# A recurrence of small matmuls woven into a projection: one burst instead of two halves in six of nine steps

## The chip, the cores and the metric

The kernel runs on one core of one Trainium2 chip. The time is device microseconds from the start to the end of one execution. Lower is better.

## The reference

One layer of a streaming encoder. 16 learned meta tokens are put ahead of 512 real tokens, the rows are RMS-normalised, and one projection `P = hn @ w_in` makes 8320 columns. Half of them feed an RWKV-7 time mixing with 16 heads of 64, the other half a gated short convolution. Both results are put side by side, go through an output projection, are added to the residual and normalised once more. The part that matters here is the recurrence, per head:

```
def step(S, inp):
    r_t, w_t, k_t, v_t, kk_t, b_t = inp
    sa = einsum('bhvk,bhk->bhv', S, kk_t)
    S = S * w_t[:, :, None, :] - sa[..., None] * b_t[:, :, None, :] + v_t[..., None] * k_t[:, :, None, :]
    y_t = einsum('bhvk,bhk->bhv', S, r_t)
    return S, y_t
```

The result `y` is then normalised per head (mean, variance), scaled and gated.

## The kernel before

The input projection is a long stream of big matmuls on TensorE: 128x128 weights against 256 to 272 or 512 columns. Every weight quarter of 512 columns is split into a high part (`nc.scalar.copy`, L149, on ScalarE) and a low part (`tensor_tensor` subtract, L150, on VectorE), and three products per weight block make up the precision. The split parts live in a pool of six buffers (`bufs=6`), so each split waits until TensorE has used up an older quarter.

TensorE's order is written out by hand, in the order in which the code issues its matmuls. The stream is a generator, `flow`; `fill(ns)` takes big matmuls from it until their costs (0.43 ns for each column) sum to at least `ns`. Everything else, the recurrence among it, is put between such fills, so that its waits lie under big matmuls. On ScalarE, VectorE, GpSimd and the DMA queue of SyncE a scheduler orders the instructions by priority, so that a change of TensorE's order can change theirs.

The recurrence (`recur`) is done in chunks of 64 tokens: nine steps, `c` from 0 (the meta tokens) to 8, with `NCH = 9`. All 16 heads go together, as 64x64 matmuls that each use a quarter of the array. One step is, in the order of TensorE:

- `rz` (L1036): products with the old state `st` and with the values. ScalarE copies the result to `pn`.
- `fill(FW["p"])`, 2900 ns of big matmuls.
- `rz` (L1053): a product with the inverse that was prepared before. ScalarE and VectorE copy the result to `u` (L1056, L1057).
- `fill(FW["u"])`, 2900 ns.
- the burst: `zs` (the update of the state, L1091) and `zy` (the output, L1095, with a part of it in `rz` at L1091) are issued in turn. In a step with both it has 160 matmuls of 64x64.
- VectorE makes the new state, `st = (zs + st) * decay` (L1103, L1104), and `norm` reduces and normalises `zy` (L1120 to L1132).
- `fill(FW["s"])`, 4200 ns, and then the next step, whose first matmuls read `st`.

In steps 1 to 7 a further `fill(FW["mid"])`, 1000 ns, stands in the middle of the burst. Steps 0 and 8 have no such fill; there the 1000 ns are added to the one after the burst:

```
if c and not last and n == steps_ // 2:
    fill(FW["mid"])
...
fill(FW["s"] if c and not last else FW["s"] + FW["mid"])
```

After the recurrence the rest of the stream runs on, and then the output projection (L1334), a Strassen-like scheme whose right-hand sides `o` are split in the same way (L1302, L1303).

Of the kernel before, what the change touches and what calls it, by code (L numbers as in the profile page):

```python
# [25 lines left out]
NCH = SEQ // CH + 1  # L26
# [16 lines left out]
FW = dict(  # L43
    evac=34, start=1062, lora=2200, gram=8800, meta={0: 2000}, gram_b=13500, gram2=5500, misc=2000, v=2000, vt=1000, solve=24500, more={0: 5500, 2: 2400},
    tr=3200, lev=3000, cp=4200, out=1500, begin=19500, p=2900, u=2900, s=4200, mid=1000, last=3700, mix=2600,
)
# [43 lines left out]
def hymba_kernel(ctx: ExitStack, tc: tile.TileContext, xt, xtok, front, w_in, w_out, pv, lup, cst, msk, gf, out):  # L90
# [512 lines left out]
    def step():  # L603
        t = next(flow, None)
        if t is None:
            run_pending(float("inf"))
        else:
            clock[0] += t
            run_pending(clock[0])
        return t  # L610

    def fill(ns):
        while ns > 0:
            seen = len(ready)
            t = step()
            if t is None:
                return
            ns -= t
            if len(ready) > seen:
                ns += FW["evac"]  # L620
# [23 lines left out]
    def ahead():  # L644
        return tc.high_priority(offset=AHEAD)
# [367 lines left out]
    def load_chunk(ch, c, pairs, ops):  # L1013
        n = OPW if c < NCH - 1 else O_B
        for i in pairs:
            t = ch.tile([P, OPW], F32, tag=f"ct{i}", name=f"ct{i}_{c}", bufs=2)
            nc.sync.dma_start(t[:, 0:n], spot(i, 0, P, c, 1, 1, 0, n))
            ops[c, i] = t
# [3 lines left out]
    def recur(ch):  # L1022
        ops = {}
        load_chunk(ch, 0, range(NPAIR), ops)
        load_chunk(ch, 1, range(NPAIR), ops)
        st = None
        for c in range(NCH):
            last = c == NCH - 1
            z = [pz.tile([P, 2, 4, CH], F32, tag="tz", name=f"rz{c}_{e}") for e in range(2)]
            for k in range(4):  # L1030
                for part in range(0 if c else 1, 2):
                    for e in range(2):
                        t = ops[c, 2 * k + e]
                        o = O_KK if part else O_AR
                        for h, hs, ho in heads:
                            nc.tensor.matmul(  # L1036
                                z[e][ho if e else hs, 0, k], t[hs, o : o + CH],
                                t[hs, O_V : O_V + CH] if part else st[hs, 4 * e + k],
                                start=(part == 0 or c == 0), stop=(part == 1),
                            )  # L1040
            pn = ch.tile([P, 2, 4, CH], F32, tag="pn", name=f"pn{c}", bufs=2)
            with ahead():
                for e in range(2):
                    nc.scalar.activation(pn[:, e], z[e][:, 0], AF.Copy, scale=-1.0)
            if c and not last:
                load_chunk(ch, c + 1, range(4, NPAIR), ops)
            fill(FW["p"])
            for k in range(4):
                for e in range(2):
                    t = ops[c, 2 * k + e]  # L1050
                    for h, hs, ho in heads:
                        m = ho if e else hs
                        nc.tensor.matmul(z[e][hs, 1, k], t[m, O_X : O_X + CH], pn[m, e, k], start=True, stop=True)  # L1053
            u = ch.tile([P, 2, 4, CH], F32, tag="u", name=f"u{c}", bufs=2)
            with ahead():
                nc.scalar.copy(u[:, 0], z[0][:, 1])  # L1056
                nc.vector.tensor_copy(u[:, 1], z[1][:, 1])  # L1057
            fill(FW["u"])
            here, there = [], []
            if not last:  # L1060
                zs = pi.tile([P, NPAIR, CH], F32, tag="misc", name=f"zs{c}")
            if c:
                zy = pi.tile([P, NPAIR - 1, CH], F32, tag="ser", name=f"zy{c}")
            for k in range(4):
                for e in range(2):
                    t, j = ops[c, 2 * k + e], 4 * e + k
                    if not last:
                        bb = t[:, O_B : O_B + 2 * CH].rearrange("p (s a) -> p a s", a=2)
                        here += [(zs, j, bb[:, 0], 0, u[:, e, k], 0, 2), (zs, j, bb[:, 1], 0, t[:, O_V : O_V + CH], 1, 2)]
                    if c and j < NPAIR - 1:  # L1070
                        there += [
                            (zy, j, st[:, j], O_AR + CH, t, 0, 3),
                            (zy, j, t[:, O_V : O_V + CH], O_KK + CH, t, 1, 3),
                            (zy, j, u[:, e, k], O_BR, t, 2, 3),
                        ]
                    elif c:

                        here += [
                            (z[0][:, 0], 0, t, O_AR + CH, st[:, j], 0, 3),
                            (z[0][:, 0], 0, t, O_KK + CH, t[:, O_V : O_V + CH], 1, 3),  # L1080
                            (z[0][:, 0], 0, t, O_BR, u[:, e, k], 2, 3),
                        ]
            steps_ = max(len(here), len(there))
            for n in range(steps_):
                if c and not last and n == steps_ // 2:
                    fill(FW["mid"])
                if n < len(here):
                    d, j, t, o, x, a, b = here[n]
                    for h, hs, ho in heads:
                        w = t[hs, o : o + CH] if o else t[hs]  # L1090
                        nc.tensor.matmul(d[hs, j], w, x[hs], start=(a == 0), stop=(a == b - 1))  # L1091
                if n < len(there):
                    d, j, x, o, t, a, b = there[n]
                    for h, hs, ho in heads:
                        nc.tensor.matmul(d[ho, j], t[hs, o : o + CH], x[hs], start=(a == 0), stop=(a == b - 1))  # L1095
            if c + 2 < NCH:
                load_chunk(ch, c + 2, range(0, 4), ops)
            if not last:
                new = ch.tile([P, NPAIR, CH], F32, tag="st", name=f"st{c}", bufs=2)
                scale = dd[:, c].unsqueeze(2).to_broadcast([P, NPAIR, CH])  # L1100
                with ahead():
                    if c:
                        nc.vector.tensor_tensor(out=new, in0=zs, in1=st, op=ALU.add)  # L1103
                    nc.vector.tensor_tensor(out=new, in0=new if c else zs, in1=scale, op=ALU.mult)  # L1104
                st = new
            if c:
                norm(ch, (zy, z[0][:, 0, 0:1]), c)
            fill(FW["s"] if c and not last else FW["s"] + FW["mid"])


    def norm(ch, zs, c):
# [40 lines left out]
    with tc.tile_pool(name="ch", bufs=1, side="right", reuse_waits="tile") as ch:  # L1152
        recur(ch)
# [463 lines left out]
```

## Time and profile before

| | |
|---|---|
| runs | 1000.02, 1000.05, 998.6 us; median 1000.02 us |
| profiled execution | 998.63 us, of which the span of instructions is 996.8 us |
| TensorE (PE) busy | 987.4 us, 99% of the span, 9767 matmuls |
| VectorE (DVE) busy | 710.1 us, 71% |
| ScalarE (ACT) busy | 389.9 us, 39% |
| GpSimd (POOL) busy | 124.6 us, 12% |
| mean granted TensorE clock | 0.998 |
| the recurrence, first to last small matmul | 623.9 to 772.5 us after the start |

PE stands for the matmuls and PEld for the loads of their weights, which overlap the matmul before. A matmul's duration runs over the start of the next one, so that the time that the stream needs is read from the distance of starts, not from the sum of durations. A merged row of the timeline ("x8") gives the start of its first instruction.

### The profile page before, as it was taken

The numbers are of one execution on the slowest core, as the hardware profiler recorded it, in microseconds if no ns is written. First come the engines' busy times: TensorE is split into PE (matmuls) and PEld (weight loads), VectorE is DVE, ScalarE is ACT, GpSimd is POOL, SyncE is SP. The second block draws the span as 40 slices with busy tenths as digits, with TensorE's granted clock in tenths as the row PEclk, the third lists the DMA queues.
The fourth block names the chain that finished last, engine by engine and source line by source line (L and its number), as shares of the span: only waits on it lengthen the run. The fifth ranks groups of instructions, "written<-read, shape, count | busy, mean of one in ns | idle before, by whom it ended". The sixth has DMA issues, their size and how long they took to land.

```text
span 996.8 us, 23828 instructions
## 1 busy us (share of the span) xinstructions
PE 987.4 (99%) x9767; PEld 911.1 (91%) x9767; DVE 710.1 (71%) x1404; ACT 389.9 (39%) x722; POOL 124.6 (12%) x234
## 2 busy tenths in 40 slices
PE   9999999999999999999999999999999999999996
PEld 9999999999998999998999998889889898788885
DVE  7777966688666678754787754455565698998897
ACT  7553422344313434323434322222232335546464
POOL 0110201102011111010111000011211102001001
PEclk9999999999999999999999999999999999999999
DMA  9426586446754374744375837777773697697654
GB/s 324 154 89 156 136 211 164 140 127 147 198 156 156 98 197 114 194 141 132 88 182 125 207 111 224 266 240 215 202 248 87 164 284 201 185 308 198 149 127 168
DMA packets 185148, 174.82 MB, mean 175 GB/s; under 512 B 121488, under 2 KB 142800, under 8 KB 184528
## 3 DMA queue, kind: packets, MB, share of 16 engines
q1 hardware_dynamic: 182448, 164.40, 56.8%
q0 software_dynamic: 2304, 8.39, 4.7%
q8 instruction: 76, 1.25, 0.5%
q10 hardware_dynamic: 288, 0.52, 0.1%
q14 instruction: 32, 0.26, 0.1%
HBM read 136.92 MB, written 36.35 MB: 174 GB/s over the span
## 4 chain that ended last, share of the span: by engine, by line
PE 95%; DVE 3%; issue 1%; ACT 0%; DMA 0%; DVEq 0%; POOL 0%; ACTq 0%
PE ps_v L350 9%; PE ps_h L350 9%; PE ps_C L350 9%; PE ps_B L365 9%; PE ps_g L350 9%; PE ps_gc L365 9%; PE ps_k L350 8%; PE ps_r L350 8%; PE M L1334 5%; PE P L1334 4%; PE Q L1334 2%; PE g L742 2%; PE ps_k L365 1%; PE zy L1095 1%; DVE o L1303 1%; PE ps_r L365 1%
## 5 line engine op out<-in xcount | busy, mean ns | idle before, releaser
L149 ACT CAST w<-wr 128x512 fp32r<-128x512 f32 x252 | 154.0, 619 | 295.5 <-PE ps_C L350 46.2
L150 DVE TENSOR_TENSOR w<-wr,w 128x512 fp32r<-128x512 f32 x252 | 178.2, 716 | 111.8 <-ACT w L149 111.1
L350 PE MATMUL ps_v<-xh,w 128*128 128x256 f32 (+2 forms) x512 | 84.1, 285 | 0.0
L365 PE MATMUL ps_B<-xh,w 128*128 128x512 f32 x256 | 83.6, 395 | 0.0
L350 PE MATMUL ps_h<-xh,w 128*128 128x256 f32 (+2 forms) x512 | 81.8, 281 | 0.0
L365 PE MATMUL ps_gc<-xh,w 128*128 128x512 f32 x256 | 81.7, 393 | 0.0
L350 PE MATMUL ps_C<-xh,w 128*128 128x256 f32 (+2 forms) x512 | 81.5, 281 | 0.0
L350 PE MATMUL ps_g<-xh,w 128*128 128x256 f32 (+2 forms) x512 | 81.5, 281 | 0.0
L350 PEld LDWEIGHTS ps_v<-xh,w 128*128 128x128 f32 x512 | 73.9, 188 | 0.3
L350 PE MATMUL ps_k<-xh,w 128*128 128x256 f32 (+1 forms) x448 | 73.6, 285 | 0.0
L350 PE MATMUL ps_r<-xh,w 128*128 128x256 f32 (+1 forms) x448 | 72.8, 281 | 0.0
L350 PEld LDWEIGHTS ps_h<-xh,w 128*128 128x128 f32 x512 | 72.0, 189 | 0.3
L350 PEld LDWEIGHTS ps_C<-xh,w 128*128 128x128 f32 x512 | 72.0, 189 | 0.4
L350 PEld LDWEIGHTS ps_g<-xh,w 128*128 128x128 f32 x512 | 72.0, 189 | 0.3
L350 PEld LDWEIGHTS ps_k<-xh,w 128*128 128x128 f32 x448 | 64.8, 188 | 0.4
L350 PEld LDWEIGHTS ps_r<-xh,w 128*128 128x128 f32 x448 | 63.6, 189 | 0.2
L350 PE MATMUL ps_h<-xl,w 128*128 128x256 f32 x256 | 56.9, 281 | 0.0
L365 PEld LDWEIGHTS ps_gc<-xh,w 128*128 128x128 f32 x256 | 47.7, 188 | 10.0
L365 PEld LDWEIGHTS ps_B<-xh,w 128*128 128x128 f32 x256 | 47.8, 188 | 9.6
L350 PE MATMUL ps_C<-xl,w 128*128 128x256 f32 x256 | 56.2, 280 | 0.0
L350 PE MATMUL ps_v<-xl,w 128*128 128x256 f32 x256 | 55.8, 278 | 0.0
L350 PE MATMUL ps_g<-xl,w 128*128 128x256 f32 x256 | 55.5, 278 | 0.0
(367 smaller groups left out, 2183.8 us busy)
## 6 DMA issues: line engine op xcount, KB each, us to landing
wr<-in_w_in_dram SPq DMA_DIRECT2D x126, 512.0 KB
ct<-opd SPq DMA_DIRECT2D x64, 288.0 KB
wo<-in_w_out_dram SPq DMA_DIRECT2D x24, 512.0 KB
x<-in_w_out_dram POOLq DMA_DIRECT2D x16, 512.0 KB, 5.7
opd<-ar SPq DMA_DIRECT2D x8, 576.0 KB
opd<-gt SPq DMA_DIRECT2D x16, 288.0 KB
opd<-bt SPq DMA_DIRECT2D x64, 64.0 KB
x<-in_w_out_dram SPq DMA_DIRECT2D x8, 512.0 KB
```

The costliest lines, as they stand in the source:

```text
L149: nc.scalar.copy(hi, rq)
L150: low[q] = eng.tensor_tensor(out=lo, in0=rq, in1=hi.bitcast(F32), op=ALU.subtract).ins
L350: nc.tensor.matmul(ps[r][:, 0 : b - a], ww[:, k * P : (k + 1) * P], xx[:, kt, a:b], start=(kt == 0 and n == 0), stop=(kt == KT - 1 and n = ...
L365: nc.tensor.matmul(ps[r], ww[:, w], xx[:, kt, a:b], start=(kt == 0 and n == 0), stop=(kt == KT - 1 and n == 2))
L742: nc.tensor.matmul(z[h][:, c - c0], bk[hs, c, h : h + 2, :].rearrange("p a s -> p (a s)"), ar[hs, c].rearrange("p a s -> p (a s)"), start= ...
L1095: nc.tensor.matmul(d[ho, j], t[hs, o : o + CH], x[hs], start=(a == 0), stop=(a == b - 1))
L1303: last = nc.vector.tensor_tensor(out=lo, in0=rq, in1=hi.bitcast(F32), op=ALU.subtract)
L1334: nc.tensor.matmul(bank[s], left(prod, jj, m, s), w, start=(jj == 0 and n == 0), stop=(jj == 7 and n == 2))
```

## The change

The fill in the middle of the burst is kept in step 7 alone (`c == NCH - 2`, the last step before the shorter last one). In steps 1 to 6 the 1000 ns move into the fill behind the burst, which asks for 5200 ns in one piece instead of 1000 and 4200.

```diff
             for n in range(steps_):
-                if c and not last and n == steps_ // 2:
+                if c == NCH - 2 and n == steps_ // 2:
                     fill(FW["mid"])
...
             if c:
                 norm(ch, (zy, z[0][:, 0, 0:1]), c)
-            fill(FW["s"] if c and not last else FW["s"] + FW["mid"])
+            fill(FW["s"] if c == NCH - 2 else FW["s"] + FW["mid"])
```

On TensorE, in the middle of the burst of step 1 (`zs` and `zy` are the burst, `ps_B` is a tile of the big stream, `st` the old state, `ct` and `u` operands of the step):

```order
@@ -2916,8 +2916,4 @@
 L1091 MATMUL zs_8670<-ct_1_8356 64x64 x2
 L1095 MATMUL zy_8671<-st_8507,ct_1_8354 64x64 x2
-L365 MATMUL ps_B_0_8562<-xh,w_8312 128x512
-L365 MATMUL ps_B_0_8562<-xh,w_8315 128x512
-L365 MATMUL ps_B_0_8562<-xl,w_8315 128x512
-L365 MATMUL ps_B_0_8562<-xh,w_8315 128x512 x2
 L1091 MATMUL zs_8670<-u_8653,ct_1_8358 64x64 x2
 L1095 MATMUL zy_8671<-ct_1_8354 64x64 x2
```

Five big matmuls leave the burst, and its two halves of 80 small ones now follow each other directly. At the end of the same burst, on TensorE:

```order
@@ -2940,4 +2936,8 @@
 L1095 MATMUL zy_8671<-ct_1_8360 64x64 x2
 L1095 MATMUL zy_8671<-u_8653,ct_1_8360 64x64 x2
+L365 MATMUL ps_B_0_8562<-xh,w_8312 128x512
+L365 MATMUL ps_B_0_8562<-xh,w_8315 128x512
+L365 MATMUL ps_B_0_8562<-xl,w_8315 128x512
+L365 MATMUL ps_B_0_8562<-xh,w_8315 128x512 x2
 L365 MATMUL ps_B_0_8562<-xl,w_8315 128x512
```

The same five stand behind the burst now. The fill there ends one big matmul of 512 columns earlier than the two fills together did (each fill runs over its sum by part of a matmul), and this one is taken later in the stream.

On VectorE, behind the same burst (`w` is a low part of the split weights, L150; `st` the new state, `nv` the first step of the norm):

```order
 L1057 COPY u_8653<-rz_1_8571 128x256
 L150 TENSOR_TENSOR w_8559<-wr_8554,w_8559 128x512
+L1103 TENSOR_TENSOR st_8760<-zs_8670,st_8507 128x512
+L1104 TENSOR_TENSOR st_8760<-st_8760,dd 128x512
+L1120 TENSOR_REDUCE nv_8763<-zy_8671 128x7
+L1120 TENSOR_REDUCE nv_8763<-rz_0_8570 128x1
 L150 TENSOR_TENSOR w_8622<-wr_8620,w_8622 128x512
-L1103 TENSOR_TENSOR st_8765<-zs_8670,st_8507 128x512
-L1104 TENSOR_TENSOR st_8765<-st_8765,dd 128x512
-L1120 TENSOR_REDUCE nv_8768<-zy_8671 128x7
-L1120 TENSOR_REDUCE nv_8768<-rz_0_8570 128x1
```

The new state and two reductions have moved ahead of one split of weights, which now stands behind instructions that wait for the end of the burst.

## The prediction

> **What bounds the kernel now.** I read the page first: the busy shares, the granted clock and the chain that ended last.
>
> ```profile
> span 996.8 us, 23828 instructions
> PE 987.4 (99%) x9767; PEld 911.1 (91%) x9767; DVE 710.1 (71%) x1404; ACT 389.9 (39%) x722; POOL 124.6 (12%) x234
> PEclk9999999999999999999999999999999999999999
> PE 95%; DVE 3%; issue 1%; ACT 0%; DMA 0%; DVEq 0%; POOL 0%; ACTq 0%
> q8 instruction: 76, 1.25, 0.5%
> ```
>
> TensorE is busy for 99% of the span and makes 95% of the chain, at full clock in every slice. Then the waits, for TensorE's matmuls over the whole span, and for its weight loads in the recurrence (620 to 775 us):
>
> ```profile
> PE pwarm L200 <- DVE cold L197: 1.0, 1, 1.0
> PE M L1334 <- DVE o L1303: 0.3, 1, 0.3
> ```
>
> ```profile
> PEld zs L1091 <- issue: 1.8, 5, 0.4
> PEld rz L1053 <- issue: 1.8, 5, 0.4
> PEld rz L1036 <- issue: 1.4, 4, 0.4
> ```
>
> No matmul of the recurrence waits for data of another engine. What is left are idle times of the weight loads of at most 0.4 us, ended by "issue", and each stands ahead of the first small matmul behind big ones. So the chip's time here is TensorE's stream, and what a change of the order can alter is the price of such changes, or a new wait. The third view is therefore the timeline of TensorE around the burst of step 2, whose halves start at 665.66 and 668.38:
>
> ```profile
> 658.57 0.39 PE L365 MATMUL ps_gc<-xl,w 128*128 128x512 f32 x1
> ...
> 661.32 0.39 PE L365 MATMUL ps_gc<-xl,w 128*128 128x512 f32 x1
> ...
> 665.66 0.28 PE L1091 MATMUL zs<-u,ct 64*64 64x64 f32 x2
> ...
> 666.83 0.23 PE L1095 MATMUL zy<-st,ct 64*64 64x64 f32 x2
> 666.85 0.23 PE L1091 MATMUL zs<-ct 64*64 64x64 f32 x2
> 667.02 0.50 PE L365 MATMUL ps_gc<-xl,w 128*128 128x512 f32 x1
> 667.35 0.62 PE L365 MATMUL ps_gc<-xh,w 128*128 128x512 f32 x2
> ...
> 668.05 0.40 PE L365 MATMUL ps_gc<-xh,w 128*128 128x512 f32 x1
> 668.38 0.28 PE L1091 MATMUL zs<-u,ct 64*64 64x64 f32 x2
> ...
> 668.49 0.23 PE L1091 MATMUL zs<-u,ct 64*64 64x64 f32 x2
> ...
> 668.55 0.23 PE L1091 MATMUL zs<-ct 64*64 64x64 f32 x2
> ...
> 669.61 0.28 PE L1095 MATMUL zy<-u,ct 64*64 64x64 f32 x4
> ```
>
> Between 658.57 and 661.32 lie twelve distances of big matmuls without a change: 2.75 us / 12 = 0.229 us each. Inside a burst four small matmuls (a row of `zs` and one of `zy`) take 0.06 us: 668.49 to 668.55.
>
> **The change part by part.** *The removed change of kinds.* At the middle of the burst TensorE goes from small to big and back. Read from those rows, against the undisturbed distances:
>
> - last small to first big: after 666.83 the next `zy` row would stand at 666.89; the big one starts at 667.02, 0.13 us late;
> - first big to second big: 667.35 - 667.02 = 0.33, 0.10 over 0.229;
> - last big to first small: 668.38 - 668.05 = 0.33, again 0.10 over;
> - first four small ones: 668.49 - 668.38 = 0.11, 0.05 over 0.06.
>
> Together 0.38 us for a split. As times are printed to 0.01 and eight of them enter, I take 0.33 to 0.44 as its bounds. A burst that starts or ends a step keeps its own changes, so exactly one pair goes for each of six steps: 6 x 0.38 = 2.28, about **2.3 us** (2.0 to 2.6). It lies on the path, since TensorE is the path. In step 3, where the stream has matmuls of 256 columns, the same gap stands:
>
> ```profile
> 684.15 0.23 PE L1091 MATMUL zs<-ct 64*64 64x64 f32 x2
> 684.31 0.39 PE L350 MATMUL ps_C<-xl,w 128*128 128x256 f32 x1
> 684.53 1.13 PE L350 MATMUL ps_C<-xh,w 128*128 128x260 f32 x8
> 685.60 0.28 PE L1091 MATMUL zs<-u,ct 64*64 64x64 f32 x2
> ```
>
> The first big one starts 0.16 us behind the last small row and holds for 0.22 us; the price does not hang on the width.
>
> [...]
>
> *The moved big matmuls.* The work is the same; five of the stream stand behind the burst instead of in it, at the same 0.229 us. The one that each longer fill no longer takes is run later, also at its usual price. Cost nothing, in sum.
>
> *The covers.* The fill ahead of the burst is unchanged, so `u` is waited for as before. The state has to be ready at the first `rz` of the next step. This is the cover that the change touches, and it grows: behind the last small matmul stands as much as 24 big ones of 512 columns instead of 20. The tightest place that the timeline shows is the end of step 4, on VectorE and TensorE:
>
> ```profile
> 705.66 0.68 DVE L1103 TENSOR_TENSOR st<-zs,st 128x512 f32<-128x512 f32 x1
> ...
> 706.92 0.68 DVE L1104 TENSOR_TENSOR st<-st,dd 128x512 f32<-128x512 f32 x1
> ...
> 708.72 0.21 DVE L1121 SCALAR_TENSOR_TENSOR yc<-nv,rz 128x64 f32<-128x64 f32 x1
> ```
>
> ```profile
> 708.98 0.39 PE L365 MATMUL ps_B<-xh,w 128*128 128x512 f32 x1
> 709.30 0.34 PE L1036 MATMUL rz<-st,ct 64*64 64x64 f32 x8
> ```
>
> The norm's last read of the `rz` bank ends at 708.72 + 0.21 = 708.93, 0.37 us ahead of the `rz` that writes it anew, and there is no wait yet: 709.30 - 708.98 is 0.32, an ordinary change of kinds. After the change the same chain starts about 4 x 0.229 = 0.9 us earlier against that `rz`. So no wait is removed, and none is due here.
>
> *The moved VectorE instructions.* In step 1 `st` and two reductions are now ahead of one split of weights (L150). Queued behind `st`, which waits for the burst's end, stand that split and the rest of the norm. TensorE waits for the split only if it is late for its quarter of the stream:
>
> ```profile
> L150 DVE TENSOR_TENSOR w<-wr,w 128x512 fp32r<-128x512 f32 x39 | 30.4, 782 | 26.2 <-ACT w L149 26.1
> ...
> L149 ACT CAST w<-wr 128x512 fp32r<-128x512 f32 x40 | 24.8, 619 | 71.7 <-PE ps_h L350 23.0 <-PE ps_gc L365 16.5 <-PE ps_C L350 14.1
> ```
>
> In 620 to 775 us the casts of the weights are busy for 24.8 us and idle for 71.7, mostly until TensorE frees a buffer. They run as far ahead as six buffers let them; one quarter feeds 12 big matmuls, 12 x 0.229 = 2.75 us, so that five quarters ahead are an estimated 13.7 us. A split that starts late by a burst of some 2.5 us stays inside that. Bounds: 0, and 0.78 us (one split) a step if that lead weren't there; I take 0, by the idle time of the casts. The DMA requests of the next chunk wait for the burst's end as before, and the burst ends earlier against the stream.
>
> The sum, against the profiled execution: 998.63 - 2.3 = 996.3 us, with a span of 994.5. Its time lies 1.4 us under the median of the runs, so against this median: 1000.02 - 2.3 = **997.7 us**.
>
> **The rivals.**
>
> *The gain is given back behind the recurrence.* TensorE reaches the output projection 2.3 us sooner; if its right-hand sides do not come sooner, it waits there. For it: in 772 to 997 us VectorE is nearly as busy as TensorE, and the weight loads of `M` have waited for it (the first row gives the stretch, its length and the busy time of PE, PEld, DVE, ACT and POOL, the other two are waits in it):
>
> ```profile
> 772.00:997.00 225.00, 216.60 (x1090) 183.21 (x1085) 191.74 (x292) 110.61 (x199) 26.84 (x31) 0.99 0.70 198
> ```
>
> ```profile
> PEld M L1334 <- DVE o L1303: 1.0, 2, 0.7
> PEld M L1334 <- ACT o L1302: 0.3, 1, 0.3
> ```
>
> Against it: VectorE's 191.7 us of 225 still leave 33 idle, these waits are 1.3 us in all, and most splits there wait for buffers that TensorE frees, so they move with it. Between half and all of the 2.3 us given back: 998.9 to 1000.0 us, no change that can be measured.
>
> *The long burst runs out of instructions, and the kernel is slower.* 160 small matmuls are 160 loads and 160 matmuls. 2 x 9767 instructions in 76 packets are 257 for each packet, and a packet takes 0.005 x 16 x 996.8 / 76 = 1.05 us. A burst in one piece would need 320 instructions in about 2.5 us, more than one packet; before, each half needed 160 and the five big matmuls between gave 1.4 us to catch up. If TensorE then stood for one packet in each of the six bursts, 6 x 1.05 = 6.3 us would come and 2.3 go: +4.0, 1004.0 us. It decides from 0.38 us of standing for each burst on. Against it: one packet's 257 instructions last 128 small matmuls, about 1.9 us at 0.06 us for four, longer than its transfer; and the longest run of small ones, step 8's 96, keeps its pace to the end (0.11 to 0.12 us for each four `zy` alone):
>
> ```profile
> 770.46 0.28 PE L1095 MATMUL zy<-st,ct 64*64 64x64 f32 x4
> 770.58 0.28 PE L1095 MATMUL zy<-ct 64*64 64x64 f32 x4
> ...
> 772.33 0.28 PE L1095 MATMUL zy<-ct 64*64 64x64 f32 x4
> 772.44 0.28 PE L1095 MATMUL zy<-u,ct 64*64 64x64 f32 x4
> ```
>
> [...]
>
> *Weights late behind the state.* The mechanism of the moved VectorE instructions, at its upper bound: 6 x 0.78 - 2.3 = +2.4, 1002.4 us. It turns the sign from the third step on in which TensorE waits for a whole split. The idle casts speak against it.
>
> **How the numbers follow.** The forecast has a chance of 0.74: every row of it is measured, and the covers grow. Giving back 0.12, instructions 0.08, late weights 0.06. A measurement of this kernel can tell about 0.2%, 2.0 us, from no change. The forecast's 2.3 us is just over that, and its bounds begin at 2.0, so I count 0.66 of its 0.74 as faster and 0.08 as within 0.2%. Faster 0.66; same 0.08 + 0.12 = 0.20; slower 0.08 + 0.06 = 0.14. The range takes the forecast and the giving back, 0.86: from the lowest run less the upper bound, 998.6 - 2.6 = 996.0, to no gain at all, 1000.0.
>
> **What would show it.** Right: in the timeline of steps 1 to 6 the 160 small matmuls stand in one piece of about 1.2 + 1.25 = 2.5 us, with one late big matmul behind them instead of two; still no wait of TensorE for VectorE or ScalarE at L1036, L1053 or L1091; and step 8's burst, 770.05 before, starts at about 766.6: 2.3 us for the changes, and five big ones (5 x 0.229 = 1.1 us) that the fills no longer take before it. Wrong: rows inside the long burst that stand further apart than 0.06 us for four (instructions), a wait of a big matmul for L150 (weights), or waits at L1334 of over 1.3 us (given back).

## The result

| | before | changed |
|---|---|---|
| median of 5 runs on one chip | 1000.05 us | 996.6 us |
| range of the runs | 998.6 to 1001.67 | 995.66 to 996.84 |
| profiled execution, span | 998.63, 996.8 us | 995.66, 993.9 us |

The ratio is 0.9968 [0.9957, 0.9979]: 3.2 us faster, between 2.1 and 4.3. Run again on another chip it was 996.34 against 998.93 us, 0.9973 [0.9963, 0.9983]: 2.6 us, so what the first runs showed beyond 2.5 us did not come again. Forecast were 997.7 us, in 996.0 to 1000.0, with 0.66 on faster.

### The profile after

The page of the changed kernel:

```profile
span 993.9 us, 23830 instructions
PE 984.5 (99%) x9767; PEld 910.2 (92%) x9767; DVE 709.2 (71%) x1404; ACT 389.7 (39%) x722; POOL 124.6 (13%) x234
PE 95%; DVE 3%; issue 1%; ACT 0%; DMA 0%; DVEq 0%; POOL 0%; ACTq 0%
```

The same matmuls, the same shares of the chain, and 2.9 us less busy time of PE: what went was priced as matmul time, as durations run over the start of the next matmul. The waits of its matmuls over the span, and of its weight loads in 620 to 775 us:

```profile
PE pwarm L200 <- DVE cold L197: 1.0, 1, 1.0
PE M L1334 <- DVE o L1303: 0.3, 1, 0.3
```

```profile
PEld rz L1053 <- issue: 1.4, 4, 0.4
PEld rz L1036 <- issue: 1.1, 3, 0.4
PEld zs L1091 <- issue: 1.1, 3, 0.4
PEld rz L1091 <- issue: 0.4, 1, 0.4
PEld rz L1036 <- PE ps_gc L365: 0.4, 1, 0.4
```

("issue" is idle time in which the engine waited for nothing that the profile shows.) Again no matmul of the recurrence waits for another engine. The same view of before has two rows more than the three that the prediction shows, put down to ScalarE's cast of the weights:

```profile
PEld zs L1091 <- ACT w L149: 0.7, 2, 0.4
PEld rz L1091 <- ACT w L149: 0.4, 1, 0.4
```

They do not upset its reading: these three idle times are 0.35 us each, as long as the "issue" ones, and stand at the same kind of place, ahead of the first small matmul behind big ones. In before there are 17 such idle times in all, in the changed kernel 12. The timeline of TensorE at the end of step 2's burst, which began at 664.55:

```profile
664.23 0.39 PE L365 MATMUL ps_gc<-xh,w 128*128 128x512 f32 x1
664.55 0.28 PE L1091 MATMUL zs<-u,ct 64*64 64x64 f32 x2
...
665.72 0.23 PE L1095 MATMUL zy<-st,ct 64*64 64x64 f32 x2
665.78 0.22 PE L1095 MATMUL zy<-ct 64*64 64x64 f32 x2
665.84 0.23 PE L1095 MATMUL zy<-ct 64*64 64x64 f32 x2
...
666.95 0.28 PE L1095 MATMUL zy<-u,ct 64*64 64x64 f32 x4
667.16 0.50 PE L365 MATMUL ps_gc<-xh,w 128*128 128x512 f32 x1
667.50 0.40 PE L365 MATMUL ps_gc<-xl,w 128*128 128x512 f32 x1
```

The burst is one piece of 667.01 - 664.55 = 2.46 us (666.95 and 0.06 for its last four), the middle included at 0.06 us for four. One change of kinds is left behind it: 667.16 - 667.01 = 0.15 late, and 667.50 - 667.16 = 0.34, 0.11 over the undisturbed 0.229.

To place the 2.9 us, I cut the span at two instructions that every kernel of this study has: the first small matmul (L1036) and the first of the output projection (L1334). In the timeline of before, and then of the changed kernel:

```profile
623.88 0.69 PE L1036 MATMUL rz<-ct 64*64 64x64 f32 x32
...
835.09 8.14 PE L1334 MATMUL M<-w,m 128*128 128x512 f32 x35
```

```profile
623.44 0.69 PE L1036 MATMUL rz<-ct 64*64 64x64 f32 x32
...
832.13 8.37 PE L1334 MATMUL M<-w,m 128*128 128x512 f32 x36
```

Call the distance R. It holds the whole recurrence and all of the stream that is left, so what a fill moves cannot change it; only changes of kinds, waits and the clock can. R went from 211.21 to 208.69 us: **2.52 us, 0.42 for each of six splits**. The other 0.44 us lie ahead of the first small matmul, in identical code, and say nothing of the change: in the second profile of the changed kernel that matmul starts at 624.81, later than before, and R is 208.69 again. Behind R, from the first matmul of the output projection to the last one of the kernel, stand 153.51 us before and 153.52 after (O below).

### The profile page after: what moved, and what is told of

Same layout as the page of the kernel before. It is cut to its first block, busy times and chain, and to the rows that moved or that the text cites. A ratio compares the mean times of both kernels' runs of the same rounds, so it can differ in the third digit from the quotient of the medians.

```text
span 993.9 us, 23830 instructions
## 1 busy us (share of the span) xinstructions
PE 984.5 (99%) x9767; PEld 910.2 (92%) x9767; DVE 709.2 (71%) x1404; ACT 389.7 (39%) x722; POOL 124.6 (13%) x234
## 4 chain that ended last, share of the span: by engine, by line
PE 95%; DVE 3%; issue 1%; ACT 0%; DMA 0%; DVEq 0%; POOL 0%; ACTq 0%
PE ps_v L350 9%; PE ps_h L350 9%; PE ps_C L350 9%; PE ps_g L350 9%; PE ps_B L365 9%; PE ps_gc L365 9%; PE ps_k L350 8%; PE ps_r L350 8%; PE M L1334 5%; PE P L1334 4%; PE Q L1334 2%; PE g L742 2%; PE ps_k L365 1%; DVE o L1303 1%; PE ps_r L365 1%; PE zs L1091 1%
## 5 line engine op out<-in xcount | busy, mean ns | idle before, releaser
L149 ACT CAST w<-wr 128x512 fp32r<-128x512 f32 x252 | 153.9, 619 | 288.1 <-PE ps_C L350 47.6
L150 DVE TENSOR_TENSOR w<-wr,w 128x512 fp32r<-128x512 f32 x252 | 177.7, 714 | 111.5 <-ACT w L149 110.7
```

Source lines behind the costliest of these rows:

```text
L149: nc.scalar.copy(hi, rq)
L150: low[q] = eng.tensor_tensor(out=lo, in0=rq, in1=hi.bitcast(F32), op=ALU.subtract).ins
```

## The experiments

R and O come from the profiled execution of each kernel; the medians from 5 to 11 runs, against 22 to 24 of before on the same chip. Each edit is against before, and those of the two rows "changed, shifted" against the changed kernel.

| kernel | median, before on that chip | ratio | R | O |
|---|---|---|---|---|
| changed, again | 996.34, 998.93 | 0.9973 [0.9963, 0.9983] | 208.69 | 153.47 |
| no split at all | 995.73, 998.53 | 0.9971 [0.9959, 0.9982] | 208.31 | 153.48 |
| split in quarters | 1003.55, 998.53 | 1.0054 [1.0040, 1.0068] | 216.11 | 153.48 |
| the 1000 ns ahead of the burst | 996.55, 998.53 | 0.9978 [0.9970, 0.9987] | 208.86 | 153.47 |
| split, long fill behind | 1000.61, 998.53 | 1.0017 [1.0009, 1.0026] | 211.46 | 155.87 |
| one big matmul between | 999.05, 998.93 | 0.9999 [0.9991, 1.0008] | 211.03 | 153.49 |
| steps 1 to 3 alone | 998.22, 998.93 | 0.9993 [0.9984, 1.0002] | 210.13 | 153.48 |
| no split, short fill behind | 1002.57, 998.93 | 1.0034 [1.0021, 1.0046] | 215.26 | 153.49 |
| changed, shifted (first) | 999.50, 999.26 | 1.0012 [1.0003, 1.0021] | 210.15 | 153.48 |
| before, shifted (first) | 1002.05, 999.26 | 1.0034 [1.0021, 1.0047] | 213.07 | 153.49 |
| changed, shifted (second) | 1000.38, 999.26 | 1.0016 [1.0007, 1.0025] | 210.71 | 153.50 |

My theory: each split costs a fixed time, the change of kinds there and back. Rivals: the time came from the longer cover behind the burst, or depends on what stands in the split.

### No split, and three

```diff
-                if c and not last and n == steps_ // 2:
+                if False:
                     fill(FW["mid"])
...
-            fill(FW["s"] if c and not last else FW["s"] + FW["mid"])
+            fill(FW["s"] + FW["mid"])
```

> Step 7's burst is in one piece too. Theory (each split costs its change of kinds and back, about 0.41 us wherever it stands): seven splits fewer than before, 7 x 0.41 = 2.9 us under the kernel before, 0.4 us under the changed one, a span of about 993.5. Rival (step 7 needs its split, since the long burst or what follows it waits there): as the changed kernel or slower, with a wait of TensorE at the first rz of step 8 or a gap inside the burst of step 7.

R fell by 2.90 us for seven splits, 0.41 each. The seventh, which the change keeps, is worth 208.69 - 208.31 = 0.38 us in the trace; the runs do not tell the two kernels apart.

```diff
-                if c and not last and n == steps_ // 2:
-                    fill(FW["mid"])
+                if c and not last and n in (steps_ // 4, steps_ // 2, 3 * steps_ // 4):
+                    fill(FW["mid"] / 3)
```

> The burst of steps 1 to 7 is in four pieces, with a third of the 1000 ns at each of three places. Theory: 14 splits more than before, 14 x 0.41 = +5.7 us. Rival (the split itself is free, and what the change gained came from the longer cover behind the burst, which is here as before): within 0.5 us of before.

R rose by 4.90 us for 14 more splits, 0.35 each, and the runs by 5.0 us, where 5.7 was expected. The direction and the size are the theory's, the price for each is at the lower end.

### Where the 1000 ns stand

```diff
-            fill(FW["u"])
+            fill(FW["u"] + FW["mid"] if 0 < c < NCH - 2 else FW["u"])
...
-                if c and not last and n == steps_ // 2:
+                if c == NCH - 2 and n == steps_ // 2:
```

> Steps 1 to 6 have their burst in one piece, but the 1000 ns go into the fill ahead of it (behind the second rz), so that the fill behind it stays at 4200 ns as before. Theory: as the changed kernel, 2.5 us under before, unless the state is late at the end of step 4 (there the slack was 0.05 us beyond the change of kinds). Rival (the gain is the longer cover of the state): within 0.5 us of before, with no gain.

The burst is in one piece, and the cover behind it stays as before. R fell by 2.35 us, nearly all of the change's 2.52. The other half of the question, the split kept and the cover lengthened:

```diff
-            fill(FW["s"] if c and not last else FW["s"] + FW["mid"])
+            fill(FW["s"] + FW["mid"])
```

> All seven splits stay as before, and the fill behind the burst is 5200 ns nevertheless, as in the changed kernel. Theory: within 0.3 us of before, since no change of kinds goes and no wait stood there. Rival (the gain is the longer cover of the state): 2.5 us under before.

R did as the theory said, +0.25 us: a longer cover brings nothing. The 0.25 us is nearly all one delay of 0.21 in the small matmuls of step 6 (at 743.55), of the kind that the last group of experiments is about. But the total missed its expectation: 2.1 us over before in the runs, 2.4 of it in O. The fills, seven times 1000 ns longer, took more of the stream into the recurrence, so that less was left behind it. The stretches between the last small matmul and the output projection, in before and then in this kernel (length, and busy time and instructions of PE, PEld, DVE, ACT, POOL):

```profile
772.70:835.08 62.38, 62.38 (x370) 55.49 (x369) 48.64 (x76) 22.13 (x40) 10.06 (x9) 1.00 0.81 225
```

```profile
779.40:834.83 55.43, 55.43 (x338) 49.71 (x338) 46.59 (x74) 21.03 (x38) 9.94 (x7) 1.00 0.76 224
```

VectorE's work in that stretch is nearly the same, 46.6 us here and 48.6 before, but it has 7 us less in which to do it, and TensorE then waits in the output projection. The three longest waits of its weight loads from 780 us on, this kernel (4.4 us in all, where before has the 1.3 that the prediction shows):

```profile
PEld M L1334 <- DVE o L1303: 2.7, 4, 1.2
PEld P L1334 <- ACT o L1302: 0.7, 1, 0.7
PEld P L1334 <- DVE o L1303: 0.4, 1, 0.4
```

So the stream behind the recurrence is itself a cover, and this kernel ate into it. The change does not: it leaves 63.5 us there.

### What stands in a split

```diff
                 if c and not last and n == steps_ // 2:
-                    fill(FW["mid"])
+                    fill(1)
...
-            fill(FW["s"] if c and not last else FW["s"] + FW["mid"])
+            fill(FW["s"] + FW["mid"])
```

> All seven splits, but with one big matmul in each instead of five or more; the fill behind the burst is 5200 ns. Theory (a split costs its two changes of kind, whatever stands between): 0.42 us for each, so as before within 0.5 us. Variant (the late second big matmul and the late first small one are one and the same delay when only one big matmul stands between): about 0.1 us less for each split, 0.7 us under before. Rival (the price is the length of the interruption): nearly nothing for each, as the kernel without splits, 2.9 us under before.

One big matmul in the middle instead of five leaves R at 211.03, 2.72 us over no split: 0.39 for each of seven. A split costs the same whether one or five stand in it. This is the strongest support for the price as a pair of changes of kinds.

```diff
-                if c and not last and n == steps_ // 2:
+                if c > 3 and not last and n == steps_ // 2:
...
-            fill(FW["s"] if c and not last else FW["s"] + FW["mid"])
+            fill(FW["s"] if c > 3 and not last else FW["s"] + FW["mid"])
```

> Only steps 1 to 3 have their burst in one piece, steps 4 to 7 keep the split. Theory (every split costs the same): half of the change's gain, 3 x 0.42 = 1.3 us under before. Rival (the gain comes from one place, the tight end of step 4): no gain, within 0.3 us of before.

Three splits gone: R fell by 1.08 us, 0.36 each, where 1.3 was expected. The runs show 0.7 us, within their uncertainty of nothing. Over these kernels a split costs 0.35 to 0.42 us.

### Whether the long burst runs out of instructions

The rival did not happen in the changed kernel. Is it far off? The first kernel leaves the fill behind the burst short, so that the long bursts stand closer together:

```diff
-                if c and not last and n == steps_ // 2:
+                if False:
                     fill(FW["mid"])
```

> No split at all, and the fill behind the burst of steps 1 to 7 stays at 4200 ns, so that some 30 big matmuls fewer run within the recurrence. Theory: the price of the changes alone counts, 2.9 us under before, as without splits and with 5200 ns; the output projection takes 153.5 us as before. Rival (with 4200 ns the state comes late where the norm and the weights share VectorE): a wait of TensorE at the first rz of step 5, and up to 1 us of the gain lost.

A miss for the theory: R rose by 4.05 us instead of falling by 2.9. The waits of TensorE's matmuls in 620 to 785 us, the timeline at the end of step 5's burst, and a table of stretches around it (the columns as above, then the granted clock and the DMA share):

```profile
PE ps_B L365 <- issue: 3.0, 1, 3.0
PE ps_C L350 <- issue: 0.7, 1, 0.7
PE rz L1053 <- ACT pn L1044: 0.4, 1, 0.4
```

```profile
715.71 0.28 PE L1095 MATMUL zy<-u,ct 64*64 64x64 f32 x4
719.03 0.73 PE L365 MATMUL ps_B<-xh,w 128*128 128x512 f32 x2 [3.04 <-issue]
```

```profile
713.00:715.80 2.80, 2.80 (x162) 2.49 (x160) 0.30 (x2) 0.00 (x0) 0.00 (x0) 1.00 0.55 145
715.80:719.00 3.20, 0.19 (x9) 0.05 (x2) 2.41 (x6) 0.00 (x0) 0.00 (x0) 1.00 0.90 292
719.00:723.50 4.50, 4.47 (x13) 3.58 (x14) 1.29 (x2) 1.15 (x2) 1.07 (x2) 0.66 0.90 346
```

The rival's wait, at the first `rz` of step 5, is not there either: the 0.4 us for data is at the second `rz`, L1053. TensorE stands for over 3 us ahead of a matmul that waits for no engine's data, at full clock, while ScalarE is idle too. The weights that it reads had long been split, as VectorE's timeline shows (712.31 + 0.69 = 713.00):

```profile
712.31 0.69 DVE L150 TENSOR_TENSOR w<-wr,w 128x512 fp32r<-128x512 f32 x1 [1.10 <-ACT w L149]
```

Behind it the granted clock is 0.66 on average: from 720.6 to 724.0 us it is halved (0.52 in that stretch), and big matmuls of 512 columns stand 0.43 us apart instead of 0.229. To see whether it lacks instructions, I count what it issued against what had come. First row below: this kernel to the end of step 5's burst. Second row: the changed kernel to the same place in the program.

```profile
0.00:715.80 715.80, 714.20 (x7727) 678.42 (x7727) 484.86 (x1054) 264.01 (x494) 91.85 (x193) 1.00 0.61 169
```

```profile
0.00:717.60 717.60, 716.42 (x7744) 680.52 (x7744) 487.79 (x1057) 264.80 (x496) 90.73 (x194) 1.00 0.61 169
```

The instruction queue of TensorE in those two stretches (packets, MB, share of 16 engines' span), and behind the first one the same queue in this kernel's 715.8 to 719.05 us:

```profile
q8 instruction: 59, 0.97, 0.5%
...
q8 instruction: 1, 0.02, 1.8%
```

```profile
q8 instruction: 60, 0.98, 0.6%
```

A load and a matmul are two instructions: 15,454 issued here on 59 packets, 262 for each packet; 15,488 there on 60, 258. At 257 to a packet, the mean over the whole kernel in the prediction, the kernel that stands is 291 ahead of its packets and the other 68. (Only loads and matmuls with a record are in the count, so only the difference, 223, counts.) One packet comes while it stands, 1.8% x 16 x 3.25 = 0.9 us long, and TensorE goes on behind it. That fits a lack of instructions, and I found no other event for which it could have waited; it is an inference from counts, not a thing that the trace names. Why the packet came so late isn't shown: the DMA engines were busy for 0.90 of that stretch, and no run separates that from a late request.

If that is right, pushing the bursts along against the packets should bring it on in the changed kernel too. These kernels add small matmuls on zeros at the start, into the tile of the warm-up (L200), from which nothing is read; their time ahead of the recurrence is not in R. Each call became two matmuls, so that 56 and 88 instructions were added, not the 28 and 44 that the expectations name, and the places that they forecast were worked out for the smaller shift.

```diff
+    for n in range(14):
+        nc.tensor.matmul(pwarm[0:CH, 0:CH], cold[0:CH, 0:CH], cold[0:CH, 0:CH], start=True, stop=True)
```

> The changed kernel with 14 matmuls of 64x64 on zeros more at its very start, 28 instructions of TensorE that move every later one against the 16 KB packets in which instructions come. Theory (a whole burst of 320 instructions lives on what is already on the core, and runs dry when it begins about 128 instructions behind a packet's boundary, as steps 5 and 7 of the kernel without splits and with 4200 ns did): the burst of step 3 now begins there, and one idle of TensorE of 0.5 to 3.3 us, ended by issue, stands behind it or behind the first big matmul after it; from the first small matmul to the output projection 209.2 to 213 us instead of 208.7. Rival (those two waits had another cause, and where instructions stand against the packets is of no weight): 208.7 us again, no idle over 0.35 us.

> The kernel before with the same 14 matmuls at its start: the control. Theory: each half of a burst needs 160 instructions and does not run dry, 211.2 us from the first small matmul to the output projection as before, no idle over 0.35 us. What the 14 matmuls themselves cost at the start, at most 1 us, is the same in both.

> The changed kernel with 22 such matmuls, 44 instructions. Theory (running dry): step 3 begins another 16 instructions later behind the boundary and still runs dry, by as much or more, unless its packet is now asked for ahead of the burst; steps 1 and 4 come closer (about 107 and 95 behind the boundary) but stay free of it. Rival: 208.7 us, no idle over 0.35 us.

The changed kernel with 14 calls: near the end of step 3's burst TensorE stands, as forecast, R +1.46 us. (About 0.4 of it is a second, shorter standing behind step 1's burst, at 657.25.)

```profile
689.36 0.28 PE L1093 MATMUL rz<-u,ct 64*64 64x64 f32 x2
690.13 0.27 PE L1093 MATMUL rz<-u,ct 64*64 64x64 f32 x1 [0.50 <-issue]
```

With 22 calls: near the end of step 4's burst, R +2.02 us. The expectation named step 3 and held step 4 to be free, a miss in the place. (A shorter one, again some 0.4 us, stands behind step 6's burst, at 739.89.)

```profile
703.09 0.28 PE L1097 MATMUL zy<-ct 64*64 64x64 f32 x3
704.40 0.27 PE L1097 MATMUL zy<-ct 64*64 64x64 f32 x1 [1.04 <-issue]
```

But before, with its halves and the same 14 calls, stands as well, behind step 6's second half and for about 0.5 us among the 32 small matmuls of step 5's second `rz` (at 715.62), R +1.86 us:

```profile
742.00 0.28 PE L352 MATMUL ps_C<-xh,w 128*128 128x256 f32 x1
743.21 0.38 PE L352 MATMUL ps_C<-xh,w 128*128 128x256 f32 x1 [0.94 <-issue]
```

The control failed its expectation, and that says more than the two others. Halves are no protection from it (0.94 us of idle behind one). The 56 instructions leave the code of the recurrence as it was and move it against the packets.

The traces hold a closer sign than the count above. There are eight such standings in the four kernels, of 0.2 to 3.0 us of idle. Up to them 12,902, 14,178, 14,944, 15,198, 15,454, 16,220 (in two kernels) and 16,730 loads and matmuls had been issued. From each of these numbers to the next it is 1276, 766, 254, 256, 766 and 510: five, three, one, one, three and two times 254 to 256, (16,730 - 12,902) / 15 = 255.2 on average, nearly the 257 for each packet. As far as the counts tell, it is always the same place in a packet. And by the packet records TensorE goes on 1.3 to 1.5 us after a packet of its queue has landed, in all eight. The delay of the kernel with the long fill behind has both marks too (16,220; 1.5 us). A wait for data has not: the 0.4 us for `pn` at L1053, above, comes at 15,042, 98 behind 14,944: 0.38 of such a distance.

The totals of the shifted kernels say little, as time goes at the start as well. In the profile of the first, the first small matmul starts at 628.64 us, 5.2 later than in the changed kernel, and at 12 us its matmuls of 512 columns still stand 0.43 us apart; in that of before with the same calls it starts 0.9 later. The expected limit of 1 us for this cost holds in the second and not in the first. With the same 14 calls the changed kernel is still 213.07 - 210.15 = 2.9 us shorter in R. What sets when a packet is asked for, and how far ahead, stays open.

## Why the prediction was right

**The removed change of kinds.** Six splits at 0.38, 2.28 us, bounds 2.0 to 2.6. Measured in R: 2.52, 0.42 each, in the upper part of the bounds. The form of the sum held too: no dependence on what stands in the split (0.39 with one big matmul), and a price that repeats over 3, 6, 7 and 14 splits at 0.36, 0.42, 0.41 and 0.35. Why it varies by a fifth was not settled; a delay such as the 0.21 us in the kernel with the long fill alone moves it by 0.04 for each of six splits and 0.07 for each of three. The interval of the runs, 2.1 to 4.3 us, contains the 2.5. That the median, 996.6 us, lies 1.1 under the forecast is not of the mechanism beyond 0.2 us: 0.44 lie ahead of the recurrence, and the rest is spread of the runs.

**The moved big matmuls.** Free, as counted. Step 8's burst, at 770.05 before, now starts at

```profile
765.96 0.27 PE L1091 MATMUL rz<-st,ct 64*64 64x64 f32 x2
```

which is 4.09 us earlier: 0.44 of the start, 2.52 of the splits, and 1.13 that are five big matmuls (5 x 0.229 = 1.15), which now run behind the recurrence. The forecast of 766.6 differs by the 0.44 and by the 0.2 that the splits were worth more.

**The covers.** The prediction listed only the waits put down to "issue" and left out two rows put down to ScalarE; they mark the same changes of kinds, so its reading holds. No new wait, and nothing gained from the longer one: without it (the 1000 ns ahead of the burst) R fell by 2.35, and the cover alone brought +0.25.

**Weights late.** TensorE's waits in the recurrence show none. The casts L149 were idle for 71.7 us before, and still for 66.3 after:

```profile
L149 ACT CAST w<-wr 128x512 fp32r<-128x512 f32 x41 | 25.3, 618 | 66.3 <-PE ps_h L350 20.5 <-PE ps_C L350 15.4 <-PE ps_B L365 14.1
```

**Given back behind the recurrence.** Not in this change: O is the same to 0.01 us, and the wait for `o` still 0.3. The mechanism exists: with 7 us less of the stream behind the recurrence it cost 2.4 us. That the change leaves slightly more there (63.5 us instead of 62.4) is on the safe side.

**The lack of instructions.** Right for this kernel, and here luck had a part: with 56 or 88 instructions more at its start the same kernel does stand. The argument against it was too weak. I took the steady pace of step 8's 96 small matmuls for a sign that 160 would hold, but bursts of the same 160 stand or not with the instructions ahead of them (R +1.46 with 56 more, +2.02 with 88), and before itself, with 80 in each half, stands with 56 more (+1.86). The price named for one standing, 1.05 us, was at the upper end of most (0.2 to 1.0 us of idle), except for the 3 us that had a granted clock of 0.66 behind it. And the point from which it decides, 0.38 us for each burst, was passed by the kernel with the short fill, which gave away its 2.9 us and 4.05 more.

## What to carry to other kernels

On an engine that is never idle, look at the distances between starts at each change from one kind of instruction to the other: here 0.35 to 0.42 us for each there-and-back, whatever stands between, so fewer and longer runs of one kind pay as long as their covers hold. Before moving filler work, see what it covers where it stood: the same 1000 ns were free ahead of the burst or behind it, but seven times 1000 ns taken from the end of the stream cost 2.4 us. Dense runs of small matmuls can, as far as these traces tell, use up the instructions that have been fetched; look for "issue" idles of up to about 1 us ahead of matmuls without data to wait for, which come and go with edits far away.

## What the hardware showed that I had not expected

TensorE stood for 0.2 to 3 us, with no data of another engine to wait for, in four kernels of this study: within or shortly behind runs of 32 to 160 small matmuls, 0.015 us each in a burst. The changed and the earlier kernel have none of it: the waits of their matmuls show no row put down to "issue", and the idle times of their weight loads in the recurrence are of at most 0.4 us.

After the 3.2 us of standing the granted clock was 0.66 over the next 4.5 us, and for 3.4 us of them the big matmuls stood 0.43 us apart instead of 0.229: this standing cost more than its own length. Behind the 1 us of the kernel with 22 calls they kept the usual distance (0.24 us, 705.54 to 705.78 in its timeline).
